# Two-layer token-mixing backbone: Fourier mixing and its merge issued beside attention A, all convolution taps on VectorE, softmax rows scaled on ScalarE

## The chip, the core and the metric

The kernel runs on one core of one Trainium2 chip. The core has five engines that work side by side, each through its own instructions in order: TensorE (PE in the profile; its weight loads are listed apart as PEld), VectorE (DVE), ScalarE (ACT), GpSimd (POOL) and SyncE (SP), which here issues the DMA transfers. The metric is the device time of one execution in microseconds (us), as the median of several runs. Lower is better.

## The reference, cut to what matters

A latent stream of 256 tokens and a context of 256 tokens, 1024 features each, pass two layers of: half a feed-forward step, token mixing, half a feed-forward step. The change lies wholly in token mixing. Four branches read the same normalised input, each result is projected to 1024 features, weighted by a sigmoid gate, and the sum goes through an output projection:

```python
def token_mixing(n, nc, ...):
    aq, ak, av, bu, cq, ck, cv, du, gl = split_cols(n @ w_in)
    ...
    y_a = blockwise(gqa_attend, qa, concat([ka, kac]), concat([va, vac]))        # A: 8 query heads, 2 kv heads
    y_c = blockwise(lambda qi, k, v: diff_attend(qi, k, v, lam), qd, ...)        # C: softmax0 - lam * softmax1, 4 heads
    y_c = diff_out(y_c, diff_subln_g, lam_init)
    y_b = conv_module(bu, ...)         # B: gated depthwise convolution over tokens, 31 taps, 512 channels, layer norm
    y_d = fourier_mix(du)              # D: real part of a 2-D FFT over tokens and the channels of 4 groups
    y = merge(y_a, y_b, y_c, y_d, gl, w_branch, w_out)
    ...                                # the context stream: the same, reading context tokens only

def merge(y_a, y_b, y_c, y_d, gate_logits, w_branch, w_out):
    y = jnp.stack([y_a, y_b, y_c, y_d], axis=2)
    proj = jnp.einsum('btnc,ncd->btnd', y, w_branch)
    g = jax.nn.sigmoid(gate_logits.reshape(gate_logits.shape[:2] + (N_BRANCH, D_MODEL)))
    return jnp.einsum('btnd,btnd->btd', g, proj) @ w_out
```

In the second layer the context's result isn't needed, so there only the latent stream is mixed (queries of 256 tokens, keys of 512).

## The kernel before, in words

Activations lie with the features on the 128 partitions and the tokens in the free dimension: 512 columns in layer 0 (latent and context, `S = 2`), 256 in layer 1 (`S = 1`). Every 128-feature product is made of three TensorE matmuls for float32 accuracy (`mm3`, L197 to L199): high and low halves of activations and weights, without low times low. Weights come from DRAM in chunks of 128x1024 (512 KB, eight 128x128 blocks), through SP's queue in the order of use; ScalarE makes the high half of a chunk (L182) and VectorE the low half (L183), the "cut" of the text.

`mixing` (L637 on) runs a layer's mixing. `win` makes one 128-wide block of the input projection (24 matmuls). The branches:
- A, for each of 4 head pairs `j` and each query tile `qt` of 128 tokens (four tiles in layer 0, two in layer 1; 16 and 8 pairs `(j, qt)`): `a_scores` (scores on TensorE L833/L834, negated maximum on VectorE L836, exponential and its sum on ScalarE L838, reciprocal on VectorE L840, `scaled` L844, for two heads), `a_turn` (transposes L849, copy L851) and `a_values` (products with the values L894). Latent tiles read 512 keys, context tiles 256. `a_q` and `a_q_turn` make the queries of a head pair (per-head norm with the small matmul L379 behind `aq_w` of L374, rope, stacking L795/L796).
- B, the convolution: for each of 4 channel blocks `b_gate`, `b_value`, then `taps`, 31 multiply-adds over shifted views. Blocks 0, 2 and 3 run on VectorE (L704, one instruction a tap); block 1 on GpSimd, a product (L700) and an addition (L702) a tap. `conv_mean` to `conv_norm` end it (the list `conv_tail`).
- C, differential attention: the same for pairs of a head `h` and a tile: `c_scores` has two score tiles, the second's reciprocal times lambda (L937), scaled (L844), and the combination of both (L939); then `c_turn`, `c_values` (L954), `c_norm`, `c_out`; `c_q` and `c_k` make the queries and keys of a head.
- D, Fourier: `f_columns` (input projection, sums and differences of token halves), `f_channels` and `f_tokens` (small matmuls), for 4 groups.
- Merge: for each branch 8 gates (`gate`, a 24-matmul product and a tanh) and four pairs of branch products (`branch`, 24 matmuls, the gated product on VectorE L988; all but the first branch are added to the sum `z` on GpSimd, L991). Then `out_proj`.

What sets the order is `spread(main, *sides)` (L90): it issues the main steps, each with a cost in units (one unit is three matmuls), and after each the share of every side list that is due by cost, so the sides stand evenly among the main work. In the first spread attention A is the side, in the second attention C, and the convolution's taps (three to a step) are a side of both. `lagged` builds a side: for pair number `i` it issues the stages with the pair that each lags by, so that a stage finds its operands ready. Within these streams a scheduler places the instructions of each engine by dependence and readiness, so the order on an engine can differ from that of the calls.

Of the kernel before, what the change touches and what calls it, by code (L numbers as in the profile page):

```python
# [12 lines left out]
AF = mybir.ActivationFunctionType  # L13
ALU = mybir.AluOpType
# [75 lines left out]
def spread(main, *sides):  # L90
    """Issues the main steps, (cost, step), and the steps of each side evenly among them."""
    total, at = sum(c for c, _ in main), 0.0
    done = [0] * len(sides)
    for c, step in main:
        step()
        at += c
        for i, side in enumerate(sides):
            upto = min(len(side), int(len(side) * at / total + 1e-6))
            for f in side[done[i]:upto]:
                f()  # L100
            done[i] = upto
# [17 lines left out]
class Build:  # L119
# [94 lines left out]
    def start(self, pool):  # L214
        """Shift and scale of the first norm for 128 features at a time; each block of features is normalised and
        multiplied with the first columns of the weights while the next one's modulation loads."""
# [72 lines left out]
    def ada(self, l, m, pool):  # L289
        """Steps over the rows of the weights for one of the modulations, and the last step."""  # L290
        nc = self.nc
        raw, st = [], {}

        def load(k):
            raw.append(self.raw([("ada_w", (l,), np.arange(128 * k, 128 * k + 128),
                                  (m * D + 32 * g + (np.arange(DB) * 128)[:, None] + np.arange(32)[None, :]).ravel())
                                 for g in range(4)], pool, "adaraw", DB - 1, False))

        def step(k):
            if k == 0:  # L300
                st["ps"] = self.aux(f"ada{l}{m}")
            for g in range(4):
                nc.tensor.matmul(st["ps"][32 * g:32 * g + 32, 0:256], self.st[:, k, :], raw[k][:, 256 * g:256 * g + 256],
                                 start=k == 0, stop=k == DB - 1)
            if k == 0:
                load(DB - 1)

        def end():
            t = self.temp(f"adat{l}{m}", 256)
            nc.vector.transpose(out=t, in_=st["ps"][:, 0:256])  # L310
            self.modulated(l, m, t.rearrange("p (b r) -> p b r", r=32)[:, :, 0:2])

        for k in range(DB - 1):
            load(k)
        return [lambda k=k: step(k) for k in range(DB)], end

    def ada_rows(self, l, ms, cond, products):
        """The same on the vector engine, outputs on the partitions: steps over blocks of 128 outputs."""
        nc = self.nc
        nc.sync.dma_start(out=cond, in_=self.cond)  # L320

        def step(m, b):
            r = self.raw([("ada_w.T", (l,), m * D + 128 * b + np.arange(128), np.arange(D))])
            for s in range(2):
                nc.vector.scalar_tensor_tensor(out=products[:, s], in0=r, scalar=1.0, in1=cond[:, s], op0=ALU.mult,  # L325
                                               op1=ALU.mult, accum_out=self.mod[l][:, m * DB + b, s:s + 1])
            if b == DB - 1:
                self.modulated(l, m, self.mod[l][:, m * DB:(m + 1) * DB, :])

        return [lambda m=m, b=b: step(m, b) for m in ms for b in range(DB)]  # L330
# [15 lines left out]
    def square(self, b, cols):  # L346
        """Squares of a block; the second step, returned, adds them to the sum over blocks."""
# [11 lines left out]
    def rstd(self, x, n, count, name, heads=1):  # L359
        """1 / sqrt(mean + eps) for each token, given squares to add up over the rows: worked out with the tokens on  # L360
        the partitions, then repeated over the 128 / heads rows of its head. The second step, returned, turns that
        back into [128, n] of PSUM."""
# [21 lines left out]
    def norm_parts(self, l, which, s, r, pooled=()):  # L384
        """Normalised and modulated features of one stream: a block's three turns on the engines."""
# [35 lines left out]
    def norm(self, l, which, s, r):  # L421
        """The same in steps; a block's turns lie a step apart."""
        pooled = (3, 6)
        start, high, low = self.norm_parts(l, which, s, r, pooled)

        def step(i):
            if i - 2 in pooled:
                low(i - 2)
            if i < DB:
                start(i)  # L430
            if 0 <= i - 1 < DB:
                high(i - 1)
            if i >= 2 and i - 2 not in pooled:
                low(i - 2)

        return [lambda i=i: step(i) for i in range(DB + 2)]
# [4 lines left out]
    def park(self, cols):  # L441
        """The residual stream waits in DRAM while its tile gathers the merged branches."""
# [4 lines left out]
    def project(self, l, m, b, block, n, x, w, h0=None, warm=False):  # L447
        """One 128-feature block of an output projection, its gated residual and squares, in steps of 8 products."""
# [19 lines left out]
    def close(self, l, m, last, block, n, x, w, h0s, closing, fill=(), fill_end=None, early=0):  # L468
        """The last blocks of an output projection, the streams apart but for the early products: the next norm of the
        latent tokens runs beside the matrix products of the context, or beside those of fill."""  # L470
# [62 lines left out]
    def context(self, l, which):  # L533
        """The context tokens' norm, in the two steps in which the matrix products of the latent ones take it in."""
# [8 lines left out]
    def halves(self, banks, widths):  # L543
        """Several column blocks, the latent tokens first; the context's norm starts beside them."""
# [72 lines left out]
    def lambdas(self):  # L617
        """For each layer: -lambda of the differential attention in column 2, the scale of its norm in column 3."""
# [18 lines left out]
    def mixing(self, l, closing):  # L637
# [5 lines left out]
        with self.tc.tile_pool(name=f"mix{l}", bufs=2) as mp:  # L643
# [24 lines left out]
            # -- B: gated depthwise convolution --  # L668
# [22 lines left out]
            def taps(i, k0, k1):  # L691
                o, yp = conv_out[i], pads[i]
                for k in range(k0, k1):
                    x, wk = yp[:, :, k:k + T], cw[:, i, k:k + 1]
                    if k == 0:
                        (nc.gpsimd if i == 1 else nc.vector).tensor_scalar(out=o, in0=x, scalar1=wk, scalar2=self.sm("conv_b", l)[:, i:i + 1],
                                                op0=ALU.mult, op1=ALU.add)
                    elif i == 1:
                        q = tl("tap", f"tap{k}", 1, (128, S, T))
                        nc.gpsimd.tensor_scalar(out=q, in0=x, scalar1=wk, scalar2=self.zero, op0=ALU.mult,  # L700
                                                op1=ALU.add)
                        nc.gpsimd.tensor_tensor(out=o, in0=o, in1=q, op=ALU.add)  # L702
# [42 lines left out]
            # -- D: Fourier mixing, radix 2 over the tokens --  # L745
# [34 lines left out]
            # -- rope on the latent half of a [128, *] block --  # L780
# [7 lines left out]
            # Two heads share a block of 128 rows. For each, its high and low parts stacked over the rows.  # L788
# [38 lines left out]
            # -- softmax rows of one query tile --  # L827
# [15 lines left out]
            def scaled(e, nk, by):  # L843
                nc.vector.tensor_scalar(out=e[:, 0:nk], in0=e[:, 0:nk], scalar1=by, scalar2=None, op0=ALU.mult)  # L844
# [9 lines left out]
            # -- A: grouped-query attention --  # L854
# [44 lines left out]
            # -- C: differential attention --  # L899
# [71 lines left out]
            # -- merge: gates and branch projections, then the output projection --  # L971
# [52 lines left out]
            # -- order: side steps lag one another so that each finds its operands ready --  # L1024
# [14 lines left out]
            side_a = lagged([(0, a_scores), (1, a_turn), (2, a_values)],  # L1039
                            {per * j - d: [lambda f=f, j=j: f(j)] for j in range(1, 4) for d, f in ((2, a_q), (1, a_q_turn))})  # L1040
            side_c = lagged([(0, c_scores), (1, c_turn), (3, c_out), (2, c_values), (2, c_norm)],
# [15 lines left out]
            def four(g):  # L1057
                return [(8, lambda: f_columns(g)), (8, lambda: f_columns(g + 1)), (8 * S, lambda: f_channels(g)),
                        (4 * S, lambda: f_tokens(g)), (8 * S, lambda: f_channels(g + 1)),
                        (4 * S, lambda: f_tokens(g + 1))]  # L1060

            spread([(8, lambda: c_q(0)), (8, lambda: c_k(0)), (8, lambda: b_gate(2)), (8, lambda: b_value(2))]
                   + four(0), side_a, conv[:2 * nconv])
            spread(merge(0, first=True) + [(8, lambda: b_gate(3)), (8, lambda: b_value(3))] + four(2) + merge(3),
                   side_c, conv[2 * nconv:3 * nconv], [lambda: None] * (3 * nconv) + conv[3 * nconv:])
            spread(merge(2), conv_tail)
# [96 lines left out]
```

## Time and profile before

| What | Value |
|---|---|
| median of 3 runs | 2295.46 us (2294.73 to 2298.6) |
| the profiled execution's span | 2292.0 us, granted TensorE clock 0.992 |
| layer 0's mixing | about 399 to 930 us |
| its first spread (with A) / second spread (with C) | about 470 to 602 / 602 to 808 us |
| layer 1's mixing | about 1741 to 2080 us |
| its first / second spread | about 1780 to 1864 / 1864 to 1978 us |
| GpSimd, busy in all | 242.9 us, of which the taps of block 1 in layer 0 76.6 us and in layer 1 53.3 us |

The profile comes from one execution: the time of each instruction, what it waited for (inferred from semaphores), and the clock that the throttle granted TensorE. The span runs from the first to the last instruction; the median of the runs is 3.5 us longer than it. Rows of instruction groups read: line of the kernel, engine, operation, output<-inputs with their shapes, count | busy us in total, mean ns of one | idle time of the engine before them, and what ended it.

### The profile page before, as it was taken

The page shows a single profiled execution, that of the slowest core. Times are in us where ns is not written, and L with a number is a line of the kernel's source. Part 1 is how long each engine was busy: PE and PEld are TensorE (multiplying, and loading weights), DVE is VectorE, ACT ScalarE, POOL GpSimd, SP SyncE. Part 2 cuts the span into 40 slices and gives each one's busy share as a digit, 9 for nine tenths or more (in the row PEclk, how much of TensorE's full clock was granted, in tenths as well). Part 3 has the DMA queues.
Part 4 walks back from the last instruction along what each step waited for, and adds up shares of the span by engine and source line. Part 5 has one row for each costly group of instructions (what it writes and reads, how often), then busy time and mean ns, then how long its engine had stood idle before and what let it go on. Part 6 is the DMA issues. An engine that isn't in the chain of part 4 may idle for free.

```text
span 2292.0 us, 32389 instructions
## 1 busy us (share of the span) xinstructions
PE 2222.7 (97%) x12822; PEld 1920.7 (84%) x12822; DVE 1505.3 (66%) x2442; ACT 923.4 (40%) x1441; POOL 242.9 (11%) x246
## 2 busy tenths in 40 slices
PE   6999999988999999999999999999999899999998
PEld 4888889866888888888888898888889889998998
DVE  6788774789758554556665545665537998766554
ACT  4322223445645443342222233223224766654443
POOL 0000000085000121110000010000001710121000
PEclk9999999989999999999999999999999999999999
DMA  8566663311122222324444423454434323455553
GB/s 319 185 205 203 200 216 116 114 56 46 48 86 71 92 92 101 111 101 156 156 155 157 154 104 126 159 165 153 158 131 168 103 90 131 157 180 170 184 183 130
DMA packets 92743, 322.82 MB, mean 141 GB/s; under 512 B 9904, under 2 KB 15280, under 8 KB 91952
## 3 DMA queue, kind: packets, MB, share of 16 engines
q1 hardware_dynamic: 92592, 320.76, 42.1%
q8 instruction: 100, 1.64, 0.3%
q14 instruction: 51, 0.42, 0.1%
HBM read 315.48 MB, written 5.24 MB: 140 GB/s over the span
## 4 chain that ended last, share of the span: by engine, by line
PE 86%; DVE 10%; issue 2%; ACT 2%; DMA 0%; POOL 0%; DVEq 0%; SPq 0%; ACTq 0%; POOLq 0%
PE p L198 12%; PE p L199 12%; PE p L197 12%; PE pr L199 6%; PE pr L198 6%; PE pr L197 6%; PE g L198 4%; PE g L199 4%; PE g L197 4%; DVE lo L183 2%; DVE cv L704 2%; PE b L197 2%; PE b L199 2%; PE b L198 2%; PE prc L199 1%
## 5 line engine op out<-in xcount | busy, mean ns | idle before, releaser
L182 ACT ACTIVATE hi<-raw 128x1024 fp32r<-128x1024 f32 x430 | 454.8, 1059 | 925.1 <-issue 319.9
L183 DVE TENSOR_TENSOR lo<-raw,hi 128x1024 fp32r<-128x1024 f32 x422 | 532.3, 1262 | 288.8 <-ACT hi L182 277.6
L197 PE MATMUL p<-nh,hi 128*128 128x512 f32 (+1 forms) x1456 | 521.0, 358 | 3.1 <-ACT hi L182 1.8
L199 PE MATMUL p<-nh,lo 128*128 128x512 f32 (+1 forms) x1456 | 520.1, 357 | 2.5 <-DVE lo L183 2.5
L198 PE MATMUL p<-nl,hi 128*128 128x512 f32 (+1 forms) x1456 | 520.4, 357 | 1.2 <-DVE nl L416 1.1
L325 DVE SCALAR_TENSOR_TENSOR prods<-raw,cond 128x1024 f32<-128x1024 f32 x240 | 288.9, 1221 | 201.0 <-DMA raw<-wst 197.8
L197 PEld LDWEIGHTS p<-nh,hi 128*128 128x128 f32 x1456 | 275.9, 190 | 44.4 <-ACT hi L182 2.4
L199 PEld LDWEIGHTS p<-nh,lo 128*128 128x128 f32 x1456 | 275.9, 189 | 42.9 <-DVE lo L183 3.7
L198 PEld LDWEIGHTS p<-nl,hi 128*128 128x128 f32 x1456 | 275.9, 189 | 41.3 <-DVE nl L416 2.1
L199 PE MATMUL pr<-gh,lo 128*128 128x512 f32 (+1 forms) x656 | 231.5, 353 | 0.0
L198 PE MATMUL pr<-gl,hi 128*128 128x512 f32 (+1 forms) x656 | 229.4, 350 | 0.0
L197 PE MATMUL pr<-gh,hi 128*128 128x512 f32 (+1 forms) x656 | 228.3, 348 | 0.0
L197 PE MATMUL g<-nh,hi 128*128 128x512 f32 (+1 forms) x512 | 175.1, 342 | 0.0
L198 PE MATMUL g<-nl,hi 128*128 128x512 f32 (+1 forms) x512 | 173.7, 339 | 0.0
L199 PE MATMUL g<-nh,lo 128*128 128x512 f32 (+1 forms) x512 | 173.3, 338 | 0.0
L198 PEld LDWEIGHTS pr<-gl,hi 128*128 128x128 f32 x656 | 123.2, 188 | 19.3
L197 PEld LDWEIGHTS pr<-gh,hi 128*128 128x128 f32 x656 | 123.6, 188 | 18.1
L199 PEld LDWEIGHTS pr<-gh,lo 128*128 128x128 f32 x656 | 123.1, 188 | 17.1
L400 POOL TENSOR_SCALAR nt<-nt,mod 128x256 f32<-128x256 f32 x18 | 12.6, 701 | 1099.4 <-DVE nt L399 1099.4
L704 DVE SCALAR_TENSOR_TENSOR cv<-yp,cw,cv 128x512 f32<-128x512 f32 (+1 forms) x180 | 119.4, 663 | 3.4
L991 POOL TENSOR_TENSOR h<-bt,h 128x512 f32<-128x512 f32 (+1 forms) x48 | 51.2, 1070 | 541.9 <-DVE bt L988 525.9
L198 PEld LDWEIGHTS g<-nl,hi 128*128 128x128 f32 x512 | 97.6, 191 | 10.3 <-issue 0.9
(429 smaller groups left out, 3695.4 us busy)
## 6 DMA issues: line engine op xcount, KB each, us to landing
raw<-wst SPq DMA_DIRECT2D x556, 512.0 KB, 3.4
adaraw<-wst SPq DMA_DIRECT2D x3, 2048.0 KB, 17.7
adaraw<-wst SPq DMA_DIRECT2D x8, 512.0 KB, 7.2
cond<-cond SPq DMA_DIRECT2D x3, 1024.0 KB, 4.7
h<-h SPq DMA_DIRECT2D x2, 1024.0 KB, 8.5
adaraw<-wst SPq DMA_DIRECT2D x2, 1024.0 KB, 11.2
parked<-h SPq DMA_DIRECT2D x8, 256.0 KB, 4.2
h<-parked SPq DMA_DIRECT2D x8, 256.0 KB, 2.6
```

Source lines behind the costliest of these rows:

```text
L182: self.nc.scalar.activation(out=hv, in_=r, func=AF.Copy)
L183: getattr(self.nc, low).tensor_tensor(out=lv, in0=r, in1=hv.bitcast(F32), op=ALU.subtract)
L197: mm(out, w[0], x[0], start=start, stop=False)
L198: mm(out, w[0], x[1], start=False, stop=False)
L199: mm(out, w[1], x[0], start=False, stop=stop)
L325: nc.vector.scalar_tensor_tensor(out=products[:, s], in0=r, scalar=1.0, in1=cond[:, s], op0=ALU.mult, op1=ALU.mult, accum_out=self.mod[l][ ...
L400: nc.gpsimd.tensor_scalar(out=t[b], in0=t[b], scalar1=scale, scalar2=shift, op0=ALU.mult, op1=ALU.add)
L704: nc.vector.scalar_tensor_tensor(out=o, in0=x, scalar=wk, in1=o, op0=ALU.mult, op1=ALU.add)
L991: nc.gpsimd.tensor_tensor(out=z[m], in0=t, in1=z[m], op=ALU.add)
```

## The change

Four edits, all in `mixing`.

Taps: block 1's first tap, its 30 products and 30 additions on GpSimd become a first tap and 30 multiply-adds on VectorE. `scaled`, one instruction for each of 72 softmax rows (48 of A, 24 of C's second score), moves from VectorE to ScalarE. The stages of `lagged` come in reverse order: for one turn, the oldest pair's stage is now issued first and the newest pair's scores last. And the main steps of the spreads are redealt:

| | before (cost units, layer 0) | after |
|---|---|---|
| first spread, beside A | `c_q(0)`, `c_k(0)`, block 2 of B, Fourier groups 0 and 1 (64 and its small products) | Fourier groups 0 to 3, merge of D with its gates (now the branch that starts the sum), block 2 of B, `c_q(0)`, `c_k(0)` (192) |
| taps beside it | blocks 0 and 1 | blocks 0 and 1 and two steps (six taps) of block 2 |
| second spread, beside C | merge of A (starts the sum), block 3 of B, Fourier groups 2 and 3, merge of D (272) | block 3 of B, merge of A (112) |
| taps beside it | block 2, then block 3 in the second half | the rest of block 2 |
| third spread | merge of C, beside `conv_tail` | merge of C, beside block 3's taps and `conv_tail` |

Merge of B with the output projection stays last. Fourier groups are also interleaved: between a group's channel products and its token products now stands the next group's input projection (a gate for the last). Comments and docstrings were taken out as well, so line numbers after are up to five smaller (L704 is L699 after, L844 is L839, now a ScalarE instruction).

```diff
                     if k == 0:
-                        (nc.gpsimd if i == 1 else nc.vector).tensor_scalar(out=o, in0=x, scalar1=wk, scalar2=self.sm("conv_b", l)[:, i:i + 1],
+                        nc.vector.tensor_scalar(out=o, in0=x, scalar1=wk, scalar2=self.sm("conv_b", l)[:, i:i + 1],
                                                 op0=ALU.mult, op1=ALU.add)
-                    elif i == 1:
-                        q = tl("tap", f"tap{k}", 1, (128, S, T))
-                        nc.gpsimd.tensor_scalar(out=q, in0=x, scalar1=wk, scalar2=self.zero, op0=ALU.mult,
-                                                op1=ALU.add)
-                        nc.gpsimd.tensor_tensor(out=o, in0=o, in1=q, op=ALU.add)
                     else:
...
             def scaled(e, nk, by):
-                nc.vector.tensor_scalar(out=e[:, 0:nk], in0=e[:, 0:nk], scalar1=by, scalar2=None, op0=ALU.mult)
+                nc.scalar.activation(out=e[:, 0:nk], in_=e[:, 0:nk], func=AF.Copy, scale=by)
...
-            side_a = lagged([(0, a_scores), (1, a_turn), (2, a_values)],
+            side_a = lagged([(2, a_values), (1, a_turn), (0, a_scores)],
...
-            side_c = lagged([(0, c_scores), (1, c_turn), (3, c_out), (2, c_values), (2, c_norm)],
+            side_c = lagged([(3, c_out), (2, c_values), (2, c_norm), (1, c_turn), (0, c_scores)],
...
-            def four(g):
-                return [(8, lambda: f_columns(g)), (8, lambda: f_columns(g + 1)), (8 * S, lambda: f_channels(g)),
-                        (4 * S, lambda: f_tokens(g)), (8 * S, lambda: f_channels(g + 1)),
-                        (4 * S, lambda: f_tokens(g + 1))]
-
-            spread([(8, lambda: c_q(0)), (8, lambda: c_k(0)), (8, lambda: b_gate(2)), (8, lambda: b_value(2))]
-                   + four(0), side_a, conv[:2 * nconv])
-            spread(merge(0, first=True) + [(8, lambda: b_gate(3)), (8, lambda: b_value(3))] + four(2) + merge(3),
-                   side_c, conv[2 * nconv:3 * nconv], [lambda: None] * (3 * nconv) + conv[3 * nconv:])
-            spread(merge(2), conv_tail)
+            def four(g, between):
+
+                def step():
+                    f_channels(g)
+                    between()
+                    f_tokens(g)
+                return (8 + 4 * S, step)
+
+            def b_block(i):
+                return [(8, lambda: b_gate(i)), (8, lambda: b_value(i))]
+
+            gates_first = merge(3, first=True)
+            fourier = [(8, lambda: f_columns(0))] + [four(g, lambda g=g: f_columns(g + 1)) for g in range(3)]
+            fourier.append(four(3, gates_first.pop(0)[1]))
+            at1, at2 = 2 * nconv + 2, 3 * nconv
+            spread(fourier + gates_first[:6] + b_block(2) + gates_first[6:] + [(8, lambda: c_q(0)), (8, lambda: c_k(0))],
+                   side_a, conv[:at1])
+            spread(b_block(3) + merge(0), side_c, conv[at1:at2])
+            spread(merge(2), conv[at2:] + conv_tail)
             spread(merge(1, last=True) + [(8, lambda b=b: out_proj(b)) for b in range(last[0])])
```

What that makes of VectorE's order around layer 0's first score rows, in the first spread. Before (`sta` are the maxima and sums of A's rows, `ea` the rows, `lo` the low halves of weights, `cqt` and `rot` the rope of C's first queries):

```order
L836 TENSOR_REDUCE sta_3635<-sa_3632 128x1
L183 TENSOR_TENSOR lo_3869<-raw_3866,hi_3868 128x1024
L783 STREAM_SHUFFLE rot<-cqt_3619 128x256
L840 RECIPROCAL sta_3635<-sta_3635 128x1
L836 TENSOR_REDUCE sta_3644<-sa_3641 128x1
L784 TENSOR_TENSOR cqt_3619<-cqt_3619,late 128x256
L785 TENSOR_TENSOR rot<-rot,late 128x256
L844 TENSOR_SCALAR ea_3637<-ea_3637,sta_3635 128x512
L786 TENSOR_TENSOR cqt_3619<-cqt_3619,rot 128x256
L840 RECIPROCAL sta_3644<-sta_3644 128x1
```

The same place after (`cv` is the convolution's block 1, `sd` the Fourier sums and differences):

```order
L696 TENSOR_SCALAR cv_3241<-yp_3584,cw,small 128x512
L699 SCALAR_TENSOR_TENSOR cv_3241<-yp_3584,cw,cv_3241 128x512 x4
L831 TENSOR_REDUCE sta_3627<-sa_3624 128x1
L183 TENSOR_TENSOR lo_3828<-raw_3825,hi_3827 128x1024
L749 TENSOR_TENSOR sd_3621<-u_3619 128x2x128
L750 TENSOR_TENSOR sd_3621<-u_3619 128x2x128
L831 TENSOR_REDUCE sta_3636<-sa_3633 128x1
L835 RECIPROCAL sta_3627<-sta_3627 128x1
L699 SCALAR_TENSOR_TENSOR cv_3241<-yp_3584,cw,cv_3241 128x512 x2
L835 RECIPROCAL sta_3636<-sta_3636 128x1
L699 SCALAR_TENSOR_TENSOR cv_3241<-yp_3584,cw,cv_3241 128x512 x7
L183 TENSOR_TENSOR lo_3966<-raw_3963,hi_3965 128x1024
```

The scale of the row and the rope of C's queries have left this place; block 1's taps, in runs, and the Fourier sums have come.

VectorE beside one pair of attention C in layer 0, in the second spread. Before (`stc` and `ec` are C's sums and rows, `ckt` the keys of the next head on their way through rope):

```order
L783 STREAM_SHUFFLE rot<-ckt_5640 128x256
L840 RECIPROCAL stc_5662<-stc_5662 128x1
L840 RECIPROCAL stc_5670<-stc_5670 128x1
L784 TENSOR_TENSOR ckt_5640<-ckt_5640,late 128x256
L785 TENSOR_TENSOR rot<-rot,late 128x256
L937 TENSOR_TENSOR stc_5670<-stc_5670,lam_77 128x1
L786 TENSOR_TENSOR ckt_5640<-ckt_5640,rot 128x256
L844 TENSOR_SCALAR ec_5672<-ec_5672,stc_5670 128x256
L939 SCALAR_TENSOR_TENSOR ec_5664<-ec_5664,stc_5662,ec_5672 128x256
```

After (`cq` are stacked queries, `cv` here block 3):

```order
L183 TENSOR_TENSOR lo_5996<-raw_5993,hi_5995 128x1024
L835 RECIPROCAL stc_5744<-stc_5744 128x1
L835 RECIPROCAL stc_5752<-stc_5752 128x1
L781 TENSOR_TENSOR cqt_5791<-cqt_5791,rot 128x256
L932 TENSOR_TENSOR stc_5752<-stc_5752,lam_77 128x1
L699 SCALAR_TENSOR_TENSOR cv_3243<-yp_5395,cw,cv_3243 128x512
L791 TENSOR_TENSOR cq_5798<-cqt_5791,cq_5798 64x512
L934 SCALAR_TENSOR_TENSOR ec_5746<-ec_5746,stc_5744,ec_5754 128x256
```

The scale between the lambda product and the combination is gone from VectorE; block 3's taps, which the calls put into the third spread, are placed here by the scheduler.

VectorE in layer 1's second spread. Before:

```order
L183 TENSOR_TENSOR lo_15666<-raw_15663,hi_15665 128x1024
L939 SCALAR_TENSOR_TENSOR ec_15521<-ec_15521,stc_15519,ec_15529 128x512
L205 TENSOR_TENSOR yl_15582<-oc_15165,yh_15581 128x256
L685 SCALAR_TENSOR_TENSOR yp_15616<-bth_15569,ba_15591 128x256
L696 TENSOR_SCALAR cv_13547<-yp_15616,cw,small 128x256
L704 SCALAR_TENSOR_TENSOR cv_13547<-yp_15616,cw,cv_13547 128x256
L183 TENSOR_TENSOR lo_15713<-raw_15710,hi_15712 128x1024
L704 SCALAR_TENSOR_TENSOR cv_13547<-yp_15616,cw,cv_13547 128x256 x5
L183 TENSOR_TENSOR lo_15749<-raw_15746,hi_15748 128x1024
```

After (`bt` are the gated products of A's merge, which GpSimd adds to the sum):

```order
L183 TENSOR_TENSOR lo_16054<-raw_16051,hi_16053 128x1024
L781 TENSOR_TENSOR ckt_15855<-ckt_15855,rot 128x256
L370 TENSOR_REDUCE cs_s<-cs_ps 128x2
L983 SCALAR_TENSOR_TENSOR bt_15949<-gt_15627,b_15936 128x256
L803 TENSOR_TENSOR ck3l_15863<-ckt_15855,ck3h_15862 64x512
L699 SCALAR_TENSOR_TENSOR cv_13487<-yp_15361,cw,cv_13487 128x256
L804 CAST ck3l_15863<-ck3l_15863 64x512
L983 SCALAR_TENSOR_TENSOR bt_15965<-gt_15752,b_15952 128x256
L831 TENSOR_REDUCE stc_15978<-sc_15975 128x1
```

Between two cuts there were a few taps; now C's keys, its norm, A's gated products and single taps of block 3 share the place.

## The prediction

> **What bounds the kernel now.** I read the page first, then the windows of the two mixing stages (layer 0 from 400 to 930 us, layer 1 from 1740 to 2080 us), then who PE waits for there, the chain of waits, and the timeline around one wait. The page:
>
> ```profile
> span 2292.0 us, 32389 instructions
> PE 2222.7 (97%) x12822; PEld 1920.7 (84%) x12822; DVE 1505.3 (66%) x2442; ACT 923.4 (40%) x1441; POOL 242.9 (11%) x246
> ```
>
> PE is the bound with 97%, so only its holes can be won: 69 us, some of them at the start. The windows (length; busy time and count of PE, weight loads, VectorE, ScalarE, GpSimd; granted clock, DMA share, GB/s) say where:
>
> ```profile
> 440.00:560.00 120.00, 101.31 (x500) 80.31 (x499) 106.61 (x162) 53.85 (x103) 78.63 (x65) 0.91 0.19 62
> 560.00:600.00 40.00, 40.00 (x285) 31.97 (x285) 35.69 (x85) 30.68 (x72) 0.00 (x0) 1.00 0.12 41
> 1780.00:1860.00 80.00, 71.75 (x532) 62.72 (x531) 73.91 (x153) 56.21 (x108) 55.30 (x63) 0.96 0.27 93
> 1860.00:1960.00 100.00, 98.32 (x735) 92.36 (x733) 90.03 (x192) 65.32 (x118) 1.02 (x2) 1.00 0.38 125
> ```
>
> In 440:560 PE is idle 120 − 101.3 = 18.7 us and works at clock 0.91, which is another 0.09 × 101.3 = 9.1 us: 27.8 us. In 1780:1860 it is 8.3 + 0.04 × 71.75 = 11.1 us, in 1860:1960 1.7 us. Together **40.6 us** that a better arrangement could return; 560:600 is full though VectorE is 89% busy there. VectorE is nearly full in both bad windows, and they are the ones in which GpSimd works. Who PE waits for in 440:560 (total, times, longest), and the chain of waits there by line:
>
> ```profile
> PE aq_ps L379 <- DVE aq_w L374: 8.8, 2, 8.0
> PE tpa L849 <- DVE sta L840: 2.3, 1, 2.3
> PE tpa L849 <- DVE ea L844: 2.2, 1, 2.2
> by line: DVE cv L704 21.2%; DVE lo L183 11.2%; issue 6.7%; DVE ea L844 6.4%; DVE sta L836 3.2%; PE ba L199 3.2%; PE ba L197 3.0%; PE ba L198 2.8%; DVE aq L796 2.8%; DVE cq L796 2.5%; PE tpa L849 2.0%; PE ck L197 1.9%; PE ck L198 1.8%; PE ck
> ```
>
> VectorE is what ends last: convolution taps, cuts of the weights into halves (L183), softmax scales (L844). What a wait costs beyond itself is in PE's timeline and its windows:
>
> ```profile
> 464.36 0.39 PE L197 MATMUL cq<-nh,hi 128*128 128x512 f32 x1
> 464.58 0.39 PE L198 MATMUL cq<-nl,hi 128*128 128x512 f32 x1
> ...
> 476.98 1.09 PE L849 MATMUL tpa<-const,ea 128*128 128x128 f32 x4 [2.24 <-DVE ea L844]
> 478.29 0.63 PE L199 MATMUL aq<-nh,lo 128*128 128x512 f32 x1
> 478.72 0.63 PE L197 MATMUL aq<-nh,hi 128*128 128x512 f32 x1
> 476.00:478.00 2.00, 1.02 (x5) 1.05 (x6) 2.00 (x2) 0.00 (x0) 1.87 (x2) 0.72 0.05 18
> 478.00:481.00 3.00, 3.00 (x10) 2.23 (x8) 2.87 (x5) 2.52 (x5) 2.76 (x3) 0.62 0.00 0
> ```
>
> 512-wide matmuls start 0.227 us apart (0.22 and 0.23 here); after the wait 0.43 apart, for about nine of them. So a 2.24 us wait costs 2.24 + 9 × 0.2 = 4.0 us.
>
> [...]
>
> **The change part by part.** (1) Taps of conv block 1 go from GpSimd to VectorE. First with GpSimd at work (440:560), then without it (taps 565:880, cuts 620:700), then layer 1's taps (1862:2050):
>
> ```profile
> L702 POOL TENSOR_TENSOR cv<-cv,tap 128x512 f32<-128x512 f32 x30 | 43.5, 1449 | 2.5
> L704 DVE SCALAR_TENSOR_TENSOR cv<-yp,cw,cv 128x512 f32<-128x512 f32 x37 | 34.1, 920 | 0.7
> L183 DVE TENSOR_TENSOR lo<-raw,hi 128x1024 fp32r<-128x1024 f32 x13 | 18.8, 1447 | 1.7 <-ACT hi L182 1.6
> ...
> L704 DVE SCALAR_TENSOR_TENSOR cv<-yp,cw,cv 128x512 f32<-128x512 f32 x41 | 30.6, 746 | 0.6
> L183 DVE TENSOR_TENSOR lo<-raw,hi 128x1024 fp32r<-128x1024 f32 x13 | 15.9, 1224 | 21.7 <-ACT hi L182 12.8 <-PE sc L834 4.5 <-PE co L954 3.5
> ...
> L704 DVE SCALAR_TENSOR_TENSOR cv<-yp,cw,cv 128x256 f32<-128x256 f32 x39 | 19.0, 487 | 0.7
> ```
>
> Added: 31 × 0.746 + 31 × 0.487 = 23 + 15 = 38 us of VectorE. Returned: 37 × 0.174 + 13 × 0.223 = 9.3 us on 52.9 us of those two groups; over all of the window's VectorE work without its scales (106.6 − 12.6 = 94) an estimate of 15. Layer 1, less exposed: an estimate of 5, by a third of that.
>
> (2) Softmax scales leave VectorE (whole run; the third row is a copy of the same shape on ScalarE):
>
> ```profile
> L844 DVE TENSOR_SCALAR ea<-ea,sta 128x512 f32<-128x512 f32 (+1 forms) x48 | 28.8, 606 | 0.6
> L844 DVE TENSOR_SCALAR ec<-ec,stc 128x512 f32<-128x512 f32 (+1 forms) x24 | 11.6, 485 | 0.5
> L203 ACT ACTIVATE yh<-oc 128x512 fp32r<-128x512 f32 x4 | 2.5, 631 | 1.0 <-DVE oc L967 1.0
> ```
>
> VectorE loses 40.4 us, ScalarE gains at most 72 × 0.631 = 45. ScalarE is at 54 of 120 and 56 of 80 in the bad windows, so it isn't the next bound; each scale is 0.63 instead of 0.49 to 0.61 on the chain of one score row, plus a handover. On VectorE (1) and (2) nearly cancel, 40.4 us away and 38 added; what it gains in all is the 20 us of contention.
>
> (3) The resequencing, the main part. Branch D's merge (8 gates, 4 pairs of branch products: 96 cost units of 3 matmuls) and two groups of Fourier columns (16 units) go from the second spread (beside attention C) to the first (beside attention A): 336 matmuls, 336 × 0.227 = 76 us of PE in layer 0 and, with a 256-wide one each 20/169 = 0.119 us, 40 us in layer 1; Fourier's own small products are 7 and 3.5 us. The merge brings 12 weight chunks with 12 cuts and 8 gate products:
>
> ```profile
> L988 DVE SCALAR_TENSOR_TENSOR h<-gt,b 128x512 f32<-128x512 f32 x8 | 5.5, 686 | 8.8 <-PE b L199 8.8
> 470.00:600.00 130.00, 112.15 (x651) 88.53 (x651) 116.39 (x207) 72.36 (x158) 74.78 (x61) 0.92 0.14 45
> 600.00:800.00 200.00, 199.62 (x999) 166.00 (x996) 134.41 (x259) 97.86 (x189) 5.20 (x4) 1.00 0.23 76
> 1870.00:1980.00 110.00, 108.32 (x816) 103.05 (x815) 94.31 (x193) 72.02 (x127) 3.62 (x5) 1.00 0.40 132
> 2040.00:2060.00 20.00, 20.00 (x169) 20.00 (x168) 12.89 (x20) 11.01 (x19) 4.42 (x6) 1.00 0.53 178
> ```
>
> VectorE's part is 12 × 1.224 + 8 × 0.686 = 20 us (layer 1: 14.7 + 8 × 0.45 = 18, the gate product scaled as the taps are), the Fourier groups' an estimate of 5.5 and 4.4 by two cuts and some adds each. Then, stage by stage, VectorE against PE at full clock:
> - Layer 0, first: PE 103 (112.15 × 0.92) + 76 + 7 = 186; VectorE 116 − 15 − 18 (about 30 scales at 0.6) + 23 + 4.5 (six taps of block 2 now also issued here) + 20 + 5.5 = 136, or **73%** instead of 90%.
> - Layer 0, second (of 200 us): PE 200 − 76 − 7 = 117; VectorE 134 − 20 − 5.5 − 8 (16 scales) = 100, **86%**.
> - Layer 1, first (1780:1860): PE 69 + 43.5 = 112; VectorE 74 − 5 − 10 + 15 + 18 + 4.4 = 96, **86%** instead of 92%.
> - Layer 1, second (1870:1980): PE 108.3 − 43.5 = 65; VectorE 94.3 − 18 − 4.4 − 4 = 68, **105%**.
>
> The moved DMAs are 12 × 0.5 MB = 6.3 MB: over 186 us 34 GB/s on top of 45 to 62, over 112 us 56 on 93. PE was full at 178 GB/s, share 0.53 (2040:2060), so loads stay hidden, with SP's queue carrying the same chunks in another order.
>
> (4) The lag reversed and main work spread differently set how many matmuls stand between a pair's scores and its transposes. For C the sequence is two maxima, two exponentials, a reciprocal, the lambda product, the scale and the combination (590:760), and PE's waits for it (602:880):
>
> ```profile
> L836 DVE TENSOR_REDUCE stc<-sc 128x1 f32<-128x512 f32 x14 | 9.1, 680 | 0.1
> L838 ACT ACTIVATE ec<-sc,stc 128x512 f32<-128x512 f32 x14 | 9.5, 686 | 7.1 <-DVE stc L836 7.1
> L838 ACT ACTIVATION_READ_ACCUMULATOR ec<-sc,stc 128x1 f32 x26 | 5.1, 198 | 0.0
> L840 DVE RECIPROCAL stc<-stc 128x1 f32<-128x1 f32 x26 | 3.8, 157 | 4.6 <-ACT ec L838 4.6
> L939 DVE SCALAR_TENSOR_TENSOR ec<-ec,stc,ec 128x512 f32<-128x512 f32 x7 | 5.2, 747 | 0.1
> PE tpc L849 <- DVE ec L939: 0.4, 1, 0.4
> ```
>
> 0.68 + 2 × 0.88 + 2 × 0.16 + 0.49 + 0.75 = 4.0 us before, 4.15 with ScalarE's 0.63, and handovers. In the order before, the closest wide C pairs of layer 0 have 4.2 us of matmuls between, and PE waited 0.4 us once: 4.2 us cover the sequence. After it, they have 4.8 to 7.6 us, so C stays covered unless VectorE's queue grows by over a microsecond.
>
> **Leftover stalls**, each bounded by 0 and by two waits of 4.0 us: layer 0 first 4 (one wait: runs of 2 and 7 block-1 taps, 7 × 0.75 = 5.2 us, now stand between the first score rows, with 4.3 us of matmuls until their transposes); layer 0 second 3 (head 3's last context tiles have 2.9 us); layer 1 first 3 (one pair with 3.4 us). Layer 1 second 7: the 3 us by which VectorE falls short, and 4 for GpSimd's merge adds, which move into it and beside which (860:960) the cuts are slower:
>
> ```profile
> L183 DVE TENSOR_TENSOR lo<-raw,hi 128x1024 fp32r<-128x1024 f32 x18 | 27.6, 1533 | 30.8 <-ACT hi L182 30.5
> ```
>
> 13 cuts × (1.533 − 1.224) = 4.0. Sum 17: the profiled span 2292.0 − 40.6 + 17 = 2268.4; the median of the runs lies 3.5 above the span, so **2272 us**.
>
> **The rivals.**
> - *All of it comes back.* VectorE at 73 to 86% waits for nobody, as in 560:600, where it was 89% busy and PE full; only layer 1's 3 + 3 us remain: 2295.5 − 40.6 + 6 = 2261. Against it: runs of taps ahead of score rows.
> - *Given back later.* The scheduler puts all of block 3's taps (23 us) into the first half of layer 0's second spread: 38 + 23 = 61 of 59 us. If PE there and in layer 1's second spread loses as in 440:560, 23% of the time, that is 14 + 15 us, with 8 left in the first spreads: 2295.5 − 40.6 + 37 = 2292. Against it: spare matmuls between scores and transposes.
> - *Slower: the denser second spread no longer covers C's scores.* The same 24 pairs stand in 117 + 65 us of PE instead of 200 + 108; if queueing on VectorE and the extra hop delay each by more than its 1 to 2 us of slack, PE waits at the transposes. If half of them pay the 4.0 us of the wait above: 2295.5 − 40.6 + 7 + 48 = 2310. It decides from nine pairs on: (40.6 − 7)/4.0 = 8.4. For it: layer 1 at 105%, block 3's crowding. Against: the 4.2 us that sufficed.
> - That the change doesn't do what it says is out: in its order GpSimd has no tap rows left, and VectorE no scales.
>
> **How the numbers follow.** Forecast 0.61, all back 0.18, given back 0.10, slower 0.11. The range takes the second and the third in, 2257 to 2293; the forecast's own is 2264 to 2282. About 0.2% (4.6 us) is what can be told from no change: faster 0.61 + 0.18 + 0.05 = 0.84; same 0.04; slower 0.12.
>
> **What would show it.** Right: clock 0.98 or more and PE idle under 3 us in the stretch after the first scores of layer 0; taps there at 0.75 us and cuts at 1.22; the aq_w wait gone; scales of 0.6 us on ScalarE; waits left mostly in layer 1's second spread, on VectorE. Wrong: PE waiting at C's transposes for the combination in many pairs, a clock under 0.95 in the second spread, or taps still at 0.9 us, since then GpSimd was not what slowed them.

## The result and the profile after

The median is 2265.98 us (2265.49 to 2266.95, four runs) against 2295.1 for the kernel before beside them: ratio 0.9872, 95% interval 0.9858 to 0.9886. That is 29.1 us faster, where 23.5 were forecast; it lies in the range. The page of the kernel after:

```profile
span 2265.2 us, 32288 instructions
PE 2216.1 (98%) x12822; PEld 1915.5 (85%) x12822; DVE 1479.9 (65%) x2432; ACT 964.6 (43%) x1513; POOL 117.7 (5%) x124
```

The windows of the two bad places and of layer 1's second spread (columns as before):

```profile
440.00:560.00 120.00, 118.78 (x653) 97.31 (x651) 86.70 (x154) 69.95 (x131) 0.36 (x4) 1.00 0.20 69
1780.00:1860.00 80.00, 77.59 (x646) 72.71 (x645) 64.64 (x136) 60.57 (x116) 0.16 (x2) 0.98 0.35 119
1860.00:1960.00 100.00, 98.17 (x691) 89.45 (x688) 91.44 (x196) 75.41 (x137) 7.27 (x8) 1.00 0.34 113
```

In 440:560 PE is idle 1.2 us instead of 18.7, and the clock is 1.00 instead of 0.91; in 1780:1860, layer 1's first spread, PE is idle 2.4 us instead of 8.3. GpSimd has no taps in any of the three; what it does in the last, 7.3 us, are additions of the merge. The groups of 440:560, and the waits of PE in layer 0's second spread (651:836):

```profile
L699 DVE SCALAR_TENSOR_TENSOR cv<-yp,cw,cv 128x512 f32<-128x512 f32 x50 | 37.5, 750 | 1.2
L183 DVE TENSOR_TENSOR lo<-raw,hi 128x1024 fp32r<-128x1024 f32 x15 | 18.3, 1219 | 11.7 <-ACT hi L182 11.7
...
L839 ACT ACTIVATE ea<-ea,sta 128x512 f32<-128x512 f32 x8 | 5.5, 718 | 0.2 <-DVE sta L835 0.2
...
PE tpc L844 <- DVE ec L934: 2.3, 3, 1.1
PE co L949 <- ACT ptc L846: 0.6, 2, 0.4
```

Taps are at 0.75 us and cuts at 1.22, as forecast; the scale is on ScalarE, where a 512-wide one takes 0.72 us (0.63 was forecast), and VectorE now waits 11.7 us for ScalarE's halves of the weights: it has room. From the start of the first key product of A to the start of the last branch product layer 0's mixing takes 525.9 us instead of 549.0, layer 1's 320.7 instead of 325.9. So all of it comes from mixing, four fifths from layer 0. Which of the edits brought it, the profile alone can't say.

### The profile page after: what moved, and what is told of

It is laid out like the page before. It is cut to its first block, busy times and chain, and to the rows that moved or that the text cites. A ratio compares the mean times of both kernels' runs of the same rounds, so it can differ in the third digit from the quotient of the medians.

```text
span 2265.2 us, 32288 instructions
## 1 busy us (share of the span) xinstructions
PE 2216.1 (98%) x12822; PEld 1915.5 (85%) x12822; DVE 1479.9 (65%) x2432; ACT 964.6 (43%) x1513; POOL 117.7 (5%) x124
## 3 DMA queue, kind: packets, MB, share of 16 engines
q8 instruction: 100, 1.64, 0.3%
## 4 chain that ended last, share of the span: by engine, by line
PE 87%; DVE 9%; ACT 3%; issue 1%; DMA 0%; POOL 0%; DVEq 0%; SPq 0%; ACTq 0%; POOLq 0%
PE p L198 12%; PE p L199 12%; PE p L197 12%; PE pr L199 7%; PE pr L198 6%; PE pr L197 6%; PE g L197 3%; PE g L198 3%; PE g L199 3%; DVE cv L699 2%; DVE lo L183 2%; PE b L197 2%; PE b L198 2%; PE b L199 2%; PE ao L889 1%
## 5 line engine op out<-in xcount | busy, mean ns | idle before, releaser
L182 ACT ACTIVATE hi<-raw 128x1024 fp32r<-128x1024 f32 x430 | 454.6, 1058 | 885.7 <-issue 250.1
L183 DVE TENSOR_TENSOR lo<-raw,hi 128x1024 fp32r<-128x1024 f32 x422 | 526.2, 1248 | 293.1 <-ACT hi L182 286.9
L699 DVE SCALAR_TENSOR_TENSOR cv<-yp,cw,cv 128x512 f32<-128x512 f32 (+1 forms) x240 | 148.7, 620 | 4.8
L197 PEld LDWEIGHTS g<-nh,hi 128*128 128x128 f32 x512 | 97.0, 189 | 10.5 <-issue 0.6
L199 PEld LDWEIGHTS g<-nh,lo 128*128 128x128 f32 x512 | 97.0, 189 | 10.4 <-issue 0.2
```

Source lines behind the costliest of these rows:

```text
L182: self.nc.scalar.activation(out=hv, in_=r, func=AF.Copy)
L183: getattr(self.nc, low).tensor_tensor(out=lv, in0=r, in1=hv.bitcast(F32), op=ALU.subtract)
L197: mm(out, w[0], x[0], start=start, stop=False)
L199: mm(out, w[1], x[0], start=False, stop=stop)
L699: nc.vector.scalar_tensor_tensor(out=o, in0=x, scalar=wk, in1=o, op0=ALU.mult, op1=ALU.add)
```

## Experiments

**Each edit alone and in pairs.** The three edits (taps on VectorE; scales on ScalarE; new order with the reversed lag) can be made apart. The diffs are those of the change, part by part.

Taps alone:

> Before, with only block 1's taps moved to VectorE. Theory V (the hole is VectorE's load in the narrow first spreads, 116 of 130 us in layer 0 and 74 of 80 in layer 1): VectorE there gets 23 and 15 us of taps and gets back 15 and 5 of contention, so it stays the bound and the time goes up by 8 + 10 to about 2313 us, unless the scheduler pushes taps into the second spread (then about 2295). Rival G (GpSimd's contention with VectorE is the hole): with GpSimd silent the taps take 0.75 and the cuts 1.22 us, and PE gets most of its holes back: 2270 to 2280.

Scales alone:

> Before, with only the softmax scales moved to ScalarE. Theory V: VectorE loses 18 of 116 us in layer 0's first spread and 10 of 74 in layer 1's, so most of the 37 us of holes there go: about 2270 us. Rival G: the taps on GpSimd go on slowing VectorE, half of the holes stay: about 2282. A third, that the longer score sequence on ScalarE costs as much as it frees: 2295.

Both, with the old order:

> Before, with both moves and the old order. Theory V: VectorE in layer 0's first spread 116 - 15 - 18 + 23 = 106 of 130 us, in layer 1's 74 - 5 - 10 + 15 = 74 of 80: part of the holes go, about 2283 us, and the new order brings the rest. Rival G: silence of GpSimd is all that was needed, about 2266, the time of the changed kernel.

The order alone:

> The changed kernel, with block 1's taps back on GpSimd and the scales back on VectorE, so only the new order and lag. Theory V: VectorE in layer 0's first spread 116 + 20 + 5.5 + 4.5 = 146 of 186 us, 79%, so its holes go even with GpSimd at work; layer 1's first 74 + 22 = 96 of 112, second 72 of 65: about 2276 us. Rival G: with GpSimd at work taps still take 0.9 us and PE still waits beside them: about 2288.

The order and the taps:

> The changed kernel with the scales back on VectorE. Theory C: the scales decide nothing, 2262 to 2268 us, as the scale run beside before showed no gain. Rival: in the denser second spreads VectorE needs the relief: 16 x 0.4 + 8 x 0.49 = 10 us more VectorE work there, about 2275.

The order and the scales:

> The changed kernel with block 1's taps back on GpSimd. Theory C: as with order alone, about 2272 us, since the stretch is covered by the wider spread only in part. Rival (scales and order together give VectorE enough slack for the contention): 2266, as the changed kernel.

All eight combinations (medians in us; ratio to the kernel before, with its interval):

| taps on | scales on | old order | new order |
|---|---|---|---|
| GpSimd | VectorE | 2295 (before) | 2272.0, 0.9896 [0.9881, 0.9911] |
| GpSimd | ScalarE | 2296.0, 1.0005 [0.9996, 1.0014] | 2268.2, 0.9883 [0.9868, 0.9897] |
| VectorE | VectorE | **2261.1**, 0.9849 [0.9832, 0.9865] | 2263.4, 0.9862 [0.9847, 0.9877] |
| VectorE | ScalarE | 2262.7, 0.9856 [0.9841, 0.9870] | 2266.0, 0.9872 [0.9858, 0.9886] (the change) |

Taps alone bring 33 us, more than the whole change: their median lies 5 us below the change's, and their slowest run (2262.0) is faster than the change's fastest (2265.5), though the intervals of the two ratios overlap. The order alone brings 22, the scales alone nothing. With the taps moved, the order reads 2.3 and 3.3 us slower and the scales 1.6 and 2.6; the intervals of these four ratios all overlap, so neither cost is told for certain. Theory V, that VectorE's load makes the holes, had 2313 for taps alone and 2270 for scales alone, and falls with both; for the order alone its 2276 was nearer than rival G's 2288. With order and scales 2268.2 lies between the 2272 and the 2266 that were expected. The windows say why V falls. First taps alone, then scales alone, both in 440:560:

```profile
440.00:560.00 120.00, 118.50 (x669) 95.03 (x668) 115.16 (x232) 72.14 (x143) 0.36 (x4) 1.00 0.21 71
...
440.00:560.00 120.00, 102.70 (x521) 80.51 (x519) 102.07 (x155) 66.59 (x129) 81.97 (x65) 0.93 0.18 60
```

With taps alone VectorE is *busier* than before, 115 of 120 us against 107, and PE is full. With scales alone VectorE is less busy, 102, and PE has its holes still: GpSimd is at 82 us. A tap there takes as long as before:

```profile
L704 DVE SCALAR_TENSOR_TENSOR cv<-yp,cw,cv 128x512 f32<-128x512 f32 x42 | 40.0, 953 | 0.7
```

The taps are filler that the scheduler puts wherever VectorE has room. With taps alone, 54 tap rows stand in layer 0's first spread and 35 in the second instead of 30 and 30, and PE is idle only 0.7 and 0.6 us there.

What the order alone does in 440:560, with GpSimd still at work:

```profile
L183 DVE TENSOR_TENSOR lo<-raw,hi 128x1024 fp32r<-128x1024 f32 x14 | 21.8, 1555 | 22.8 <-ACT hi L182 22.8
L704 DVE SCALAR_TENSOR_TENSOR cv<-yp,cw,cv 128x512 f32<-128x512 f32 x20 | 15.0, 750 | 0.5
```

Cuts are stretched beside GpSimd, from 1.22 to 1.56 us, but taps are not. The trace shows why: no tap of VectorE runs between 460 and 603 us, and GpSimd works through block 1 from 466 to 544. Before, 13 taps ran in 466:550, at 1.24 us each. So the new order does two things at once: it gives VectorE less to do in that time (79 rows in 466:550 instead of 101, 51.7 us busy instead of 72.2), and it keeps VectorE's taps away from GpSimd's.

**GpSimd's rows left out.** Nothing of VectorE's rows changes; block 1's convolution is only its first tap, so its products and additions are not computed:

```diff
                     elif i == 1:
-                        q = tl("tap", f"tap{k}", 1, (128, S, T))
-                        nc.gpsimd.tensor_scalar(out=q, in0=x, ...)
-                        nc.gpsimd.tensor_tensor(out=o, in0=o, in1=q, op=ALU.add)
+                        pass
```

> Before, with the 60 product and addition rows of conv block 1 on GpSimd left out in each layer (its output is then only the first tap). VectorE's own rows are those of before. Theory C (contention: GpSimd's rows stretch VectorE's, and a queue planned without slack falls behind): 2255 to 2263 us, no better than taps on VectorE by more than 5. Rival V (VectorE's own load makes the holes): 2290 to 2295.

It takes 2256.7 us (ratio 0.9838, 0.9821 to 0.9854), within theory C's 2255 to 2263. The window from the first scores of A to the first of C in layer 0, before and then here:

```profile
469.80:602.10 132.30, 114.45 (x675) 90.28 (x673) 117.15 (x209) 73.79 (x162) 74.98 (x61) 0.92 0.14 45
...
468.90:575.30 106.40, 105.87 (x675) 84.33 (x673) 91.50 (x209) 73.50 (x162) 0.00 (x0) 1.00 0.16 56
```

This is the clearest pair of rows in the study. The same 675 matmuls and the same 209 VectorE instructions stand in both. Beside GpSimd the 209 take 117.2 us, without it 91.5: contention costs VectorE 25.7 us, and the spread is 25.9 us longer. What VectorE loses here, PE loses, nearly one for one. So it is over the whole run: the same 2442 VectorE instructions take 1505.3 us before and 1468.3 here, 37.0 us less, and the kernel is 37.5 us faster than the one before beside it.

**GpSimd busy for nothing.** The kernel with taps alone, and beside each tap of block 1 GpSimd works into a scratch tile that nothing reads: products and additions, products alone, or additions alone.

```diff
                     else:
                         nc.vector.scalar_tensor_tensor(out=o, in0=x, scalar=wk, in1=o, ...)
+                        if i == 1:
+                            q = tl("tap", f"tap{k}", 1, (128, S, T))
+                            nc.gpsimd.tensor_scalar(out=q, in0=x, scalar1=wk, scalar2=self.zero, ...)
+                            nc.gpsimd.tensor_tensor(out=q, in0=x, in1=q, op=ALU.add)
```

> The kernel with taps on VectorE, and beside them GpSimd still does as many products and additions (60 a layer, into a scratch tile that nothing reads). Theory C: VectorE has the most rows of all and each is stretched again (taps at 0.9 us): the holes come back and more, 2300 to 2330 us. Rival P (the kernel with taps on VectorE is faster because the scheduler placed VectorE's rows in another order, not because GpSimd is silent): about 2262.

> Taps on VectorE, and beside them only the 30 products a layer on GpSimd (one input tile, result in a scratch tile that nothing reads); the 30 additions are left out. Theory C by time: each GpSimd row stretches whatever VectorE row with SBUF inputs meets it, so the cost goes with GpSimd's busy time, 33 of 77 us in layer 0: about 2261 + 0.45 x 41 = 2280 us. Rival (only GpSimd rows with two inputs collide): 2262.

> Taps on VectorE, and beside them only 30 additions a layer on GpSimd (two inputs, scratch result); the products are left out. Theory C by time: about 2261 + 0.55 x 41 = 2284 us. Rival (only rows with two inputs collide): the whole 41 us, about 2300.

Measured: 2302.1 us with both (ratio 1.0034, 1.0021 to 1.0047), 2272.5 with products (0.9906, 0.9891 to 0.9921), 2286.9 with additions (0.9970, 0.9958 to 0.9981). Against 2261.1 without, GpSimd's useless work costs 41, 11 and 26 us. Rival P, that only the placing of VectorE's rows helped, is out. In 440:560, with both, with products, with additions:

```profile
L699 DVE SCALAR_TENSOR_TENSOR cv<-yp,cw,cv 128x512 f32<-128x512 f32 x51 | 48.9, 968 | 0.8
...
L699 DVE SCALAR_TENSOR_TENSOR cv<-yp,cw,cv 128x512 f32<-128x512 f32 x64 | 50.4, 796 | 0.8
L702 POOL TENSOR_SCALAR tap<-yp,cw,zero 128x512 f32<-128x512 f32 x30 | 37.0, 1232 | 9.1 <-DVE yp L685 6.2
...
L699 DVE SCALAR_TENSOR_TENSOR cv<-yp,cw,cv 128x512 f32<-128x512 f32 x58 | 49.1, 855 | 0.7
L702 POOL TENSOR_TENSOR tap<-yp 128x512 f32<-128x512 f32 x30 | 40.1, 1336 | 8.5 <-DVE yp L685 6.2
```

A tap is 0.75 us alone, 0.80 beside products, 0.86 beside additions, 0.97 beside both. The cost does not go with GpSimd's busy time: 37 and 40 us of it cost 11 and 26. Nor do only GpSimd's rows with two inputs collide: products cost 11 too. By busy time theory C had 2280 and 2284; additions come within 3 us of it, products 7.5 below, and the ratio of the two costs, 11 to 26, is not that of the times. What the cost does go with is how much VectorE's rows are lengthened. The pages of taps alone, products, additions and both list the same 2504 VectorE instructions:

```profile
PE 2211.8 (98%) x12822; PEld 1913.3 (85%) x12822; DVE 1496.0 (66%) x2504; ACT 923.5 (41%) x1441; POOL 110.7 (5%) x124
PE 2217.2 (98%) x12822; PEld 1918.1 (84%) x12822; DVE 1506.2 (66%) x2504; ACT 924.2 (41%) x1441; POOL 175.3 (8%) x184
PE 2219.6 (97%) x12822; PEld 1919.7 (84%) x12822; DVE 1521.5 (67%) x2504; ACT 923.9 (40%) x1441; POOL 174.1 (8%) x184
PE 2223.8 (97%) x12822; PEld 1921.6 (84%) x12822; DVE 1537.0 (67%) x2504; ACT 923.9 (40%) x1441; POOL 242.4 (11%) x244
```

VectorE's busy time grows by 10.2, 25.5 and 41.0 us, and the kernel by 11, 26 and 41: one for one, with one profiled execution of each. Why an addition lengthens VectorE's rows more than a product does stays open.

**The reversed lag of attention C undone.** In the changed kernel:

```diff
-            side_c = lagged([(3, c_out), (2, c_values), (2, c_norm), (1, c_turn), (0, c_scores)],
+            side_c = lagged([(0, c_scores), (1, c_turn), (3, c_out), (2, c_values), (2, c_norm)],
```

> The changed kernel with attention C's lag in its old sequence (scores first, the oldest pair last). Theory L (the reversed lag leaves C's pairs too few matmuls between scores and transposes, which makes the 3.2 us of waits in layer 0's second spread): those waits go, 2263 us. Rival (VectorE is short there whatever the sequence): 2266 as the changed kernel; or, with four rows' buffers held longer, slower than it by a few us.

2264.5 us (0.9871, 0.9856 to 0.9885), the change's time within the noise. PE's waits in layer 0's second spread:

```profile
PE cs_ps L379 <- DVE cs_w L374: 0.9, 1, 0.9
PE sc L828 <- ACT ck1h L802: 0.7, 1, 0.7
```

The waits of the transposes (`tpc`) are gone, 2.3 us, as theory L had it, and 1.6 us of others have come, at the norm and the keys. PE's idle time in this spread falls from 3.2 to 1.6 us, and layer 0's mixing from 525.9 to 523.7. So half of what theory L named came back in this one execution; the medians are too close to show it.

**The best of each layer.** The old order in layer 0 and the new one in layer 1 (chosen by the layer's number), taps and scales on VectorE in both:

> Taps on VectorE and scales on VectorE in both layers, the old order and lag in layer 0, the new order and lag in layer 1. By the stages of the runs so far (layer 0's mixing 523.1 us with taps alone, 527.4 with taps and the new order; layer 1's 319.1 and 317.7) about 1.4 us below taps alone: 2259.7. Rival (one lucky execution each): 2261 to 2263.

2260.7 us (2258.0 to 2262.6), against 2261.1 (2260.1 to 2262.0) with taps alone: no difference that can be told. No run of either is as slow as the fastest of the change (2265.5); taps alone is the smaller edit.

## Why the prediction came out right, and where its steps were wrong

The total fell in the range, but in part by luck. The change holds two remedies for one hole, taps off GpSimd and the new order, and the forecast credited mostly the second; either brings more than 20 us alone, so the sum came near whichever of them was at work. Of the 6 us by which it missed, 3.2 lie in the span (2268.4 forecast, 2265.2 measured) and 2.7 in the step from span to median: 3.5 us were added for it, 0.8 was measured.

- **Where the time was.** Right: 40.6 us were put into 440:560 and 1780:1960. By the same count (PE's idle time and the clock) 26.6 us came back in 440:560 and 7 in 1780:1860, and layer 0's second spread lost some 3.
- **"What bounds": wrong in the step from busy to bound.** "VectorE is nearly full in both bad windows, and they are the ones in which GpSimd works" names two suspects, and the sums went on with the first. VectorE at 96% with PE full (taps alone) shows that its share says little: much of it is filler that can wait. The second suspect was the cause, as the 209 equal rows and the one-for-one costs of GpSimd's useless work show.
- **Part 1 (taps): the sign right, the place in the sum wrong.** Contention was an estimate of 15 in layer 0 (its own ratio, 9.3 of 52.9 us on 94, gives 16.5); it is 25.7 in the first spread, and 37.0 over both layers where 20 were forecast. And the added taps, 23 us of them in that spread, were charged against it as if they took room that PE's work needed; with taps alone 24 of the 30 stand there, VectorE is busy 104.0 of its 108.6 us, and PE is idle 0.7.
- **Part 2 (scales): price nearly right, worth wrong.** 40.4 us away from VectorE and at most 45 on ScalarE were forecast; the 72 rows there take 45.8 (30.2 and 15.6 in the groups of the whole run). But alone they free nothing that PE waited for: 0 us, and with taps the medians read 1.6 to 2.6 us slower (beside the order alone 3.8 faster, with overlapping intervals). What a scale on ScalarE can cost is seen in layer 1 of the change: PE's longest wait there, 2.0 us at A's transposes, is for a scale that stands behind the high half of a weight chunk (L182, 1.06 us) in ScalarE's order, and the clock falls after it (0.91 in 1780:1800). With order and taps but the scales on VectorE neither is there, and layer 1's mixing takes 317.7 us instead of 320.7; layer 0's takes 527.4 instead of 525.9.
- **Part 3, "the main part": the step that failed.** The new order does cover the holes: with GpSimd still at work and the cuts still stretched, 22 of the 33 us come back, by the wider spread and by the taps that no longer meet GpSimd's (how much by each isn't shown). As a cover it works. But with taps moved there is nothing left to cover, and the median reads 2.3 us slower; by the stages it is 4.4 us in layer 0, whose second spread then has PE waiting for C, with 1.4 given back in layer 1. The forecast put reliefs of VectorE that fix the same hole into one sum and called the order the main part; the eight combinations show that order and taps replace one another.
- **Leftover stalls, by PE's idle time in each stage: 17 forecast, about 10 measured.** Layer 0 second 3 and 3.2 (right, but the longest wait, 1.1 us, was at a wide tile). Layer 0 first 4 and 0.4; runs of seven taps ahead of a score row held up nobody. Layer 1 first 3 and 2.5, with 1.7 more for the clock. Layer 1 second 7 and 2.3, where VectorE at a sum of 105% was no bound for the same reason as above, and the 4.0 us for cuts beside GpSimd's merge additions did not come: they take 1.25 us there, not 1.53. The price of 4.0 us a wait was too high for short ones: of the waits left in layer 0, none over 1.1 us, none slowed the clock, which is 1.00 in every window of 40 us there. For the one of 2.0 us in layer 1 it was about right: 2.0 and 1.7 for the clock. By an estimate from these numbers, without the clock's 1.8 of every 4.0 us in layer 0's 4 and 3 the forecast would have been 3 us lower, and nearer.
- **The rivals.** "All of it comes back" (2261) is the time of taps alone, though not of the change and not by its reason: there VectorE is at 96%. The slower one did not come: its waits are the three `tpc` waits above, 2.3 us in layer 0's 16 pairs. The wait of 8.0 us for `aq_w`, the longest before, is gone. The test that counted stood at the very end of the prediction, as what would clear GpSimd: taps that stay at 0.9 us with GpSimd silent. They did not stay there.

## What to carry to other kernels

A busy engine is not yet the bound: ask which of its rows can wait, and compare the duration of *one* row in the bad window with the same row elsewhere. Where the same instructions are longer beside a second engine, silence that engine first (leave its rows out in a trial run) before redealing the order: one such run would have named the cause here. Edits that fix the same hole don't add up; try each alone, and keep the one that removes the cause rather than those that cover it.

## What the runs showed of the hardware

What GpSimd does to VectorE can be seen row by row. GpSimd's and VectorE's timelines of the kernel before:

```profile
505.36 1.27 POOL L702 TENSOR_TENSOR cv<-cv,tap 128x512 f32<-128x512 f32 x1
506.74 1.08 POOL L700 TENSOR_SCALAR tap<-yp,cw,zero 128x512 f32<-128x512 f32 x1
507.91 2.11 POOL L702 TENSOR_TENSOR cv<-cv,tap 128x512 f32<-128x512 f32 x1
510.12 1.09 POOL L700 TENSOR_SCALAR tap<-yp,cw,zero 128x512 f32<-128x512 f32 x1
...
505.46 1.72 DVE L796 TENSOR_TENSOR aq<-aq01t,aq 64x512 fp32r<-64x512 f32 x1
507.21 1.68 DVE L183 TENSOR_TENSOR lo<-raw,hi 128x1024 fp32r<-128x1024 f32 x1
508.93 1.64 DVE L796 TENSOR_TENSOR aq<-aq01t,aq 64x512 fp32r<-64x512 f32 x1
510.59 0.16 DVE L840 RECIPROCAL sta<-sta 128x1 f32<-128x1 f32 x1
510.67 0.67 DVE L836 TENSOR_REDUCE sta<-sa 128x1 f32<-128x512 f32 x1
```

A stacking row of 0.69 us takes 1.72 and 1.64 beside GpSimd's rows, and a cut 1.68 instead of 1.22, while the maximum, which reads PSUM, takes its usual 0.67 beside the last product (also the mean of the ten wide ones in 440:560, against 0.68 there with taps alone); what spares it isn't shown. GpSimd is held up too: the addition that meets the cut takes 2.11 us, the one before it 1.27. In these three VectorE rows the penalty is half a microsecond to one, and the cut, the longest of them, has the least. Scales, which read one tile, are lengthened too: a 512-wide one takes 0.48 us in 440:560 with taps alone and 0.88 before. The experiments add the price: additions lengthen VectorE's rows by 25.5 us and products by 10.2, for 40 and 37 us of GpSimd in layer 0.
